# Modulation vectors by plain float32 matmuls in four 32-column strips, with nine early weight blocks in flight

## The chip, the core and the metric

The kernel runs on one core of a Trainium2 chip. Its engines are TensorE (PE, with its weight loads shown apart as PEld), VectorE (DVE), ScalarE (ACT), GpSimd (POOL) and SyncE (SP, which issues the transfers). Each engine takes its instructions in the order in which they were written for it, and waits for others through semaphores. The metric is device microseconds of one execution; lower is better.

## The reference, cut to what matters

Two layers of a generator's backbone run over 1024 latent tokens and 256 context tokens of width 1024. Each layer begins with a modulation: two conditioning vectors (one for the latents, `c`, one for the context, `c_ctx`) go through silu and a 1024 x 3072 weight, and give a shift, a scale and a gate per feature. The normed tokens are scaled and shifted with them before the layer's big input projection.

```python
for l in range(DEPTH):                      # DEPTH = 2
    mod = jax.nn.silu(c) @ w_mod[l] + b_mod[l]
    modc = jax.nn.silu(c_ctx) @ w_mod[l] + b_mod[l]
    shift, scale, gate = jnp.split(mod[:, None, :], 3, axis=-1)
    shift_c, scale_c, gate_c = jnp.split(modc, 3, axis=-1)
    h = rmsnorm(x, g_pre[l]) * (1.0 + scale) + shift
    hc = rmsnorm(xc, g_pre[l]) * (1.0 + scale_c) + shift_c
    u, uc = even_mixer(h, hc, ...) if l % 2 == 0 else odd_mixer(h, hc, ...)
    x = x + gate * rmsnorm(u @ w_out[l], g_post[l])
```

## The kernel before

**Products in float32r.** A matmul of the type fp32r streams a column per step of PE, but keeps fewer bits of its operands. So the kernel splits every operand of its large products into a high and a low part, and adds three products (high x high, high x low, low x high). A weight block is 128 x 1024 numbers, 512 KB. `load_w` (L223) has SP fetch it into `wraw`; `split_w` has ACT cast it into `whi` (L237) and POOL, or for some blocks DVE, subtract that from `wraw` into `wlo` (L238).

**The stream of weights.** `Stream` holds the weight blocks (`Unit`) in the order of their use. When a unit begins, `prefetch` loads the next three and splits the next one. There are three buffers for `wraw` and two for `whi` and `wlo`. The units of the first modulation (`early`) have a pool of their own, with four raw and three split buffers; six of them are loaded and two split ahead.

**The modulation.** `mod_units` computes 256 columns of one layer's modulation from two units of 512 x 256 numbers. `sst` holds the two silu vectors split in high and low, four columns for each of eight groups of 128 rows; it is the stationary operand (128 x 128, of which four columns matter), and the weight block is the moving one. A step (one unit) is eight fp32r matmuls of 256 columns, four on `whi` and four on `wlo` (L264), into one PSUM tile `modps`, whose rows 0 to 3 are the sums. `mod_flush` runs inside the next step or projection chunk: twice it copies four rows of 128 to SBUF (`modrow`, L282, DVE) and transposes them on PE (`modtr`, L283), then it adds them into columns (L285, L288). The layer's eight shift and scale blocks of layer 0 (16 units) come at the very start; the other 16 blocks (32 units: layer 0's gates, all of layer 1) stand in layer 0's stream, two blocks for each of the eight heads.

**The start.** `start` loads the first four token tiles, then the 16 modulation blocks, then further token tiles between the first weights of the projections. `make_h` turns the normed tokens into `h`: for each group of 128 features four transposes (`xtr`, L344), scale and shift (`ht`, L350 on DVE or L348 on ACT), cast (`hAh`, L351, ACT), subtraction (`hAl`, L352, DVE or POOL). Part A of `h` is tokens 0 to 511; part B (`hBh`, `hBl`) is tokens 512 to 1023 and the 256 of the context. The first projections (`pj`, L433; 24 matmuls for a chunk of tokens) start when A is there, and B is made beside them. DVE and POOL also turn the first results with the rotary tables (`ropex`).

**Layer 0's heads.** For each head, score matmuls (`S`), a softmax, transposes of the weights (`atr`, L606, evacuated by ACT and by DVE into `ath` and `atl`, L610) and value matmuls (`av`) are woven with the projections of the next head and of a convolution (`cacc`: L661 scales 1280 columns on DVE, L664 and L665 add the neighbours).

**What sets the order.** A scheduler of the kernel language decides, by its own estimates, in which order the instructions of each engine are written; after that the order is fixed. Outside the start and the neighbourhoods of the modulation steps in the eight heads, the change leaves that order as it was.

Of the kernel before, what the change touches and what calls it, by code (L numbers as in the profile page):

```python
# [31 lines left out]
class Unit:  # L32
    """a weight tile and the steps of the tensor engine that use it."""

    def __init__(self, name, src, steps, width=P, lo=None, pool=None):
        self.name, self.src, self.steps, self.width, self.lo_eng, self.pool = name, src, list(steps), width, lo, pool
        self.raw = self.hl = None
        self.hold = self.extra = False
        self.early = pool is not None


class Stream:
    """the weights in the order of their use: loaded two tiles ahead, split into hi and lo one tile ahead.
    A plain string in the order is a gate that stays shut until open() is called with it."""
# [4 lines left out]
    def ahead(self, n):  # L49
        """the next n units."""  # L50
        while sum(isinstance(u, Unit) for u in self.q) < n:
            u = next(self.units, None)
            if u is None:
                break
            self.q.append(u)
        return [u for u in self.q if isinstance(u, Unit)][:n]

    def prefetch(self, n=1):
        for i, u in enumerate(self.ahead(7)):
            if i < (6 if u.early else 3):  # L60
                self.K.load_w(u)
            if i < (2 if u.early else n):
                self.K.split_w(u)
# [37 lines left out]
class Kernel:  # L101
# [20 lines left out]
    def setup(self):  # L122
# [21 lines left out]
        self.sst = c.tile([P, 4 * NK + 124], F32R, name="sst")  # L144
# [15 lines left out]
    def turn_small(self, pool, rows, cols, name):  # L160
        """pieces of 128 numbers, each a row, into columns."""
# [10 lines left out]
    def setup_cond(self, p):  # L172
        """silu of the two conditioning vectors, split: columns c_hi, ctx_hi, c_lo, ctx_lo of each k."""
# [4 lines left out]
        sil = p.tile([P, 16], F32, name="sil")  # L178
        self.silu2(sil, self.colsA[:, 0:16])
        nc.vector.tensor_scalar_mul(sil, sil, 0.5)  # L180
        nc.vector.memset(self.sst.bitcast(F32), 0.0)
        sv = sil.rearrange("p (s k) -> p k s", s=2)
        s4 = self.sst[:, 0:4 * NK].rearrange("p (k s) -> p k s", s=4)
        nc.vector.tensor_copy(s4[:, :, 0:2], sv)
        nc.vector.tensor_tensor(out=s4[:, :, 2:4], in0=sv, in1=s4[:, :, 0:2].bitcast(F32), op=ALU.subtract)

    def setup_rest(self, p):
# [4 lines left out]
        # halves for the gates, which come as 2 silu  # L192
# [15 lines left out]
    def silu2(self, out, x):  # L208
        """2 silu(x) = x (1 + tanh(x / 2))."""
# [15 lines left out]
    def w_room(self, u, what=0):  # L225
        pool, *bufs = (self.prepw, 4, 3) if u.pool else (self.wp, 3, 2)
# [14 lines left out]
    def units(self):  # L241
        """every weight tile in the order of its use."""
        for j in (0, 4, 1, 5, 2, 6, 3, 7):
            yield from self.mod_units(0, j, "vp", (True, j > 3))
# [7 lines left out]
    def mod_units(self, l, j, lo=None, prep=None):  # L252
        """columns 256 j .. 256 j + 256 of mod(l), for latents and context."""
        st = {}

        def step(i):
            def f(hi, lo):
                nc = self.nc
                if i == 0:
                    st["ps"] = self.ps_pj.tile([P, 512], F32, name="modps", tag="pj")  # L260
                ps = st["ps"]
                for n, w in enumerate((hi, lo)):
                    for k in range(4):
                        nc.tensor.matmul(ps[:, 0:256], lhsT=self.sst[:, 16 * i + 4 * k:16 * i + 4 * k + P], rhs=w[:, k, :],  # L264
                                         start=i + n + k == 0, stop=i == n == 1 and k == 3)
                self.mod_flush()
                if i == 1:
                    self.mod_todo = (l, j, ps)
            return f

        for i in range(2):
            yield Unit(f"mod{l}.{j}.{i}", self.A["w_mod"][l][512 * i:512 * i + 512, 256 * j:256 * j + 256], [step(i)], 256, lo and lo[i], prep and prep[i])

    def mod_flush(self):
        """the last block's sums into columns."""
        if self.mod_todo is None:
            return
        nc, (l, j, ps), self.mod_todo = self.nc, self.mod_todo, None
# [23 lines left out]
    def rstd(self, r, t, ms, scale=1.0):  # L302
        """r from scale ms, with a step of Newton's behind the two tables; t is scratch."""
# [1303 lines left out]
```

## Time and profile before

| | |
|---|---|
| median of three runs | 3145.3 us (3143.07 to 3146.52) |
| span of the profiled execution | 3144.7 us |
| PE busy | 2961.4 us, 94% of the span |
| DVE, ACT, POOL busy | 62%, 49%, 35% |
| first projection matmul | 61.03 us |
| modulation matmuls | 384, of 256 columns |

PE is busy almost throughout, apart from the first 105 us. "Busy" of a matmul includes its way through the array, so that consecutive ones overlap: the distance between starts says what one costs. The granted clock is given in shares of full speed, 2.4 GHz; 0.50 is the lower level, 1.2 GHz.

### The profile page before, as it was taken

The page shows a single profiled execution, that of the slowest core. Times are in us where ns is not written, and L with a number is a line of the kernel's source. Part 1 is how long each engine was busy: PE and PEld are TensorE (multiplying, and loading weights), DVE is VectorE, ACT ScalarE, POOL GpSimd, SP SyncE. Part 2 cuts the span into 40 slices and gives each one's busy share as a digit, 9 for nine tenths or more (in the row PEclk, how much of TensorE's full clock was granted, in tenths as well). Part 3 has the DMA queues.
Part 4 walks back from the last instruction along what each step waited for, and adds up shares of the span by engine and source line. Part 5 has one row for each costly group of instructions (what it writes and reads, how often), then busy time and mean ns, then how long its engine had stood idle before and what let it go on. Part 6 is the DMA issues. An engine that isn't in the chain of part 4 may idle for free. (4 is left out here: it accounts for less than half of the span.)

```text
span 3144.7 us, 42660 instructions
## 1 busy us (share of the span) xinstructions
PE 2961.4 (94%) x16196; PEld 2480.0 (79%) x16196; DVE 1954.2 (62%) x3352; ACT 1547.3 (49%) x2809; POOL 1109.3 (35%) x851
## 2 busy tenths in 40 slices
PE   5999999999999999999999989989899999999898
PEld 4788888888888888787877777777778888887786
DVE  6774756656575757566254586776845666667723
ACT  5553535444454535464254465655534555556521
POOL 4323131212222231315233243443435555556522
PEclk8999999999999999999999999999999999999999
DMA  6011111102111111114343112121231111113323
GB/s 223 28 41 51 34 58 41 51 28 64 34 52 39 43 49 34 49 43 174 118 141 108 44 33 63 38 71 38 68 99 40 43 43 43 43 44 95 105 97 121
DMA packets 236983, 206.59 MB, mean 66 GB/s; under 512 B 43591, under 2 KB 194538, under 8 KB 236778
## 3 DMA queue, kind: packets, MB, share of 16 engines
q1 hardware_dynamic: 236778, 203.87, 20.7%
q8 instruction: 127, 2.08, 0.3%
q14 instruction: 78, 0.64, 0.1%
HBM read 168.17 MB, written 35.67 MB: 65 GB/s over the span
## 5 line engine op out<-in xcount | busy, mean ns | idle before, releaser
L238 POOL TENSOR_TENSOR wlo<-wraw,whi 128x1024 fp32r<-128x1024 f32 x189 | 459.6, 2434 | 1123.9 <-ACT whi L237 842.5
L237 ACT CAST whi<-wraw 128x1024 fp32r<-128x1024 f32 x224 | 234.5, 1049 | 327.7 <-PE ops L748 175.1
L433 PE MATMUL pj<-hBh,whi 128*128 128x512 f32 (+1 forms) x1712 | 386.0, 353 | 1.0 <-ACT gk L1035 1.0
L433 PE MATMUL pj<-hBl,whi 128*128 128x512 f32 (+1 forms) x1712 | 366.2, 346 | 0.0
L433 PE MATMUL pj<-hBh,wlo 128*128 128x512 f32 (+1 forms) x1712 | 353.3, 344 | 0.0
L433 PEld LDWEIGHTS pj<-hBh,wlo 128*128 128x128 f32 x1712 | 278.9, 190 | 37.4
L433 PEld LDWEIGHTS pj<-hBl,whi 128*128 128x128 f32 x1712 | 276.0, 190 | 34.6
L433 PEld LDWEIGHTS pj<-hBh,whi 128*128 128x128 f32 x1712 | 273.8, 190 | 34.3 <-ACT gk L1035 1.2
L433 PE MATMUL pj<-hAh,whi 128*128 128x512 f32 x968 | 275.5, 408 | 15.0 <-ACT ropex L511 11.9
L433 PE MATMUL pj<-hAl,whi 128*128 128x512 f32 x968 | 258.6, 398 | 0.0
L586 DVE TENSOR_REDUCE st<-S 128x1 f32<-128x1280 f32 (+1 forms) x160 | 203.9, 1275 | 80.5 <-PE S L584 79.4
L433 PE MATMUL pj<-hAh,wlo 128*128 128x512 f32 x968 | 248.2, 392 | 0.0
L1438 POOL TENSOR_TENSOR np<-np,nst 128x640 f32<-128x640 f32 x128 | 166.6, 1304 | 192.2 <-DVE nst L1437 143.7
L588 ACT ACTIVATE p<-S,st 128x1280 f32<-128x1280 f32 (+1 forms) x160 | 185.9, 1162 | 85.9 <-DVE st L586 85.1
L433 PEld LDWEIGHTS pj<-hAh,wlo 128*128 128x128 f32 x968 | 179.7, 188 | 36.3
L433 PEld LDWEIGHTS pj<-hAl,whi 128*128 128x128 f32 x968 | 180.2, 191 | 35.5
L433 PEld LDWEIGHTS pj<-hAh,whi 128*128 128x128 f32 x968 | 171.6, 191 | 44.2 <-ACT ropex L511 13.5
L584 PE MATMUL S<-kst,qd 128*128 128x512 f32 (+1 forms) x832 | 194.1, 363 | 0.6 <-ACT p L588 0.2
L584 PEld LDWEIGHTS S<-kst,qd 128*128 128x128 f32 x832 | 140.4, 191 | 40.2 <-ACT p L588 19.1
L1434 DVE CUSTOM_DVE_ANT_0 np<-NS,nB 128x640 f32<-128x640 f32 x128 | 105.3, 823 | 91.2 <-PE NS L1431 85.3
L609 ACT CAST ath<-atr 128x512 fp32r<-128x512 f32 (+1 forms) x208 | 99.1, 504 | 125.8 <-PE atr L606 124.8
L1489 DVE TENSOR_TENSOR ptl<-ntr,pth 128x512 fp32r<-128x512 f32 (+2 forms) x224 | 117.5, 536 | 49.0 <-ACT pth L1488 45.1
(361 smaller groups left out, 6384.2 us busy)
## 6 DMA issues: line engine op xcount, KB each, us to landing
wraw<-in_ev_w_in_dram SPq DMA_DIRECT2D x64, 512.0 KB, 4.1
wraw<-in_od_w_in_dram SPq DMA_DIRECT2D x56, 512.0 KB, 3.9
wraw<-in_w_out_dram SPq DMA_DIRECT2D x55, 512.0 KB, 3.7
wraw<-in_w_mod_dram SPq DMA_DIRECT2D x48, 512.0 KB, 3.6
sgT<-gt SPq DMA_DIRECT2D x32, 256.0 KB, 2.0
uT<-sg SPq DMA_DIRECT2D x8, 640.0 KB, 2.9
nG<-in_rpbp_dram SPq DMA_DIRECT2D x128, 40.0 KB, 2.2
xt<-in_x_dram SPq DMA_DIRECT2D x8, 512.0 KB, 6.2
```

Source lines behind the costliest of these rows:

```text
L237: nc.scalar.copy(out=hi, in_=u.raw)
L238: (nc.vector if u.lo_eng == "v" else nc.gpsimd).tensor_tensor(out=lo, in0=u.raw, in1=hi.bitcast(F32), op=ALU.subtract)
L433: nc.tensor.matmul(ps[:, 0:tn], lhsT=a[:, k, :], rhs=self.h_at(k, t0, tn)[b], start=n == 0, stop=n == 23)
L584: nc.tensor.matmul(S[:, c0:c0 + tn], lhsT=qd[:, 2 * m + part, P * qt:P * qt + P], rhs=self.kst[m][:, t0:t0 + tn], start=part == 0, stop=pa ...
L586: nc.vector.tensor_reduce(out=st[:, m:m + 1], in_=S[:, 0:n], axis=AX.X, op=ALU.max, negate=True)
L588: nc.scalar.activation(out=p[m][:, 0:n], in_=S[:, 0:n], func=AF.Exp, bias=st[:, m:m + 1], accum_out=st[:, 2 + m:3 + m])
L609: nc.scalar.copy(out=dh, in_=tv)
L1434: nc.vector.tensor_tensor_reduce(out=p, in0=S[:, z0:z0 + 640], in1=bias[2 * i + m][:, c0:c0 + 640], scale=1.0, scalar=3e38, op0=ALU.add, o ...
L1438: nc.gpsimd.tensor_tensor(out=p, in0=p, in1=st[:, 2:3].broadcast_to([P, 640]), op=ALU.mult)
L1489: nc.vector.tensor_tensor(out=lv[:, s:e], in0=tr[:, s:e], in1=hv[:, s:e].bitcast(F32), op=ALU.subtract)
```

## The change

The modulation's units become `plain`: they are not split. The raw float32 block is the moving operand of float32 matmuls. `sst` now holds, for each of the eight groups of 128 rows, 32 columns of which two are the silu vectors and 30 are zero. A step is four matmuls with a stationary operand of 32 columns; the k-th writes to PSUM partitions 32 k to 32 k + 31, that is, it takes the k-th strip of 32 columns of the array. The two steps of a block accumulate, strip by strip. DVE then copies all 128 rows at once (128 x 256), and two float32 matmuls with that copy as the stationary operand and `sel` (128 x 2; column s is one on the rows 32 k + s) as the moving one add the four strips and turn rows into columns. The copy stands at the end of a block's second step, the two matmuls ahead of the next step's (or behind the next projection chunk's). The early units get nine raw buffers and eight are loaded ahead.

```diff
     def prefetch(self, n=1):
-        for i, u in enumerate(self.ahead(7)):
-            if i < (6 if u.early else 3):
+        for i, u in enumerate(self.ahead(9)):
+            if i < (8 if u.early else 3):
                 self.K.load_w(u)
-            if i < (2 if u.early else n):
+            if i < n and not u.early:
                 self.K.split_w(u)
...
+        self.sel = c.tile([P, 2], F32, name="sel")
+        nc.vector.tensor_reduce(out=self.sel, in_=self.ident.rearrange("p (j x) -> p x j", x=32)[:, 0:2, :], axis=AX.X, op=ALU.add)
...
+    def new_sst(self, pool, eng):
+        self.sst = pool.tile([P, NK, 32], F32, name="sst")
+        eng.memset(self.sst, 0.0)
+        eng.tensor_copy(self.sst[:, :, 0:2], self.sil)
...
-        pool, *bufs = (self.prepw, 4, 3) if u.pool else (self.wp, 3, 2)
+        pool, *bufs = (self.prepw, 9, 0) if u.early else (self.wp, 3, 2)
...
+        if u.plain:
+            u.hl = u.raw.rearrange("p (k n) -> p k n", n=u.width),
+            return
...
-            def f(hi, lo):
+            def f(w):
                 nc = self.nc
+                self.mod_flush()
                 if i == 0:
                     st["ps"] = self.ps_pj.tile([P, 512], F32, name="modps", tag="pj")
                 ps = st["ps"]
-                for n, w in enumerate((hi, lo)):
-                    for k in range(4):
-                        nc.tensor.matmul(ps[:, 0:256], lhsT=self.sst[:, 16 * i + 4 * k:16 * i + 4 * k + P], rhs=w[:, k, :],
-                                         start=i + n + k == 0, stop=i == n == 1 and k == 3)
-                self.mod_flush()
+                for k in range(4):
+                    nc.tensor.matmul(ps[32 * k:32 * k + 32, 0:256], lhsT=self.sst[:, 4 * i + k, :], rhs=w[:, k, :], start=i == 0, stop=i == 1)
                 if i == 1:
-                    self.mod_todo = (l, j, ps)
+                    row = self.rowp.tile([P, 256], F32, name="modrow", tag="modrow")
+                    nc.vector.tensor_copy(row, ps[:, 0:256])
+                    self.mod_todo = (l, j, row)
...
         for i in range(2):
-            row = self.const.tile([16, P], F32, name="modrow", tag="modrow")[0:4]
-            nc.vector.tensor_copy(row, ps[0:4, P * i:P * i + P])
-            nc.tensor.transpose(out=tr[:, 4 * i:4 * i + 4], in_=row, identity=self.ident[0:4, 0:4])
-        tc_ = self.const.tile([P, 8], F32, name="modtc", tag="modtc", bufs=2)
-        nc.vector.tensor_copy(tc_, tr[:, 0:8])
-        for i in range(2):
-            m = 2 * j + i
-            nc.vector.scalar_tensor_tensor(out=self.modT[l][:, m, :], in0=tc_[:, 4 * i:4 * i + 2], scalar=self.b_mod(l)[:, m:m + 1],
-                                           in1=tc_[:, 4 * i + 2:4 * i + 4], op0=ALU.add, op1=ALU.add)
+            nc.tensor.matmul(tr[:, 2 * i:2 * i + 2], lhsT=row[:, P * i:P * i + P], rhs=self.sel, start=True, stop=True)
+        m = slice(2 * j, 2 * j + 2)
+        nc.vector.tensor_tensor(out=self.modT[l][:, m, :], in0=tr[:, 0:4].rearrange("p (m s) -> p m s", s=2),
+                                in1=self.b_mod(l)[:, m].rearrange("p (m o) -> p m o", o=1).broadcast_to([P, 2, 2]), op=ALU.add)
```

PE's order at the start, before (line 264 is a modulation matmul, 283 a transpose of its sums, 344 a transpose of tokens):

```order
L264 MATMUL modps<-whi,sst 128x256 x4
L264 MATMUL modps<-wlo,sst 128x256 x4
L264 MATMUL modps<-whi,sst 128x256 x4
L264 MATMUL modps<-wlo,sst 128x256 x4
L264 MATMUL modps<-whi,sst 128x256 x4
L264 MATMUL modps<-wlo,sst 128x256 x4
L283 MATMUL modtr<-ident,modrow 128x4
L264 MATMUL modps<-whi,sst 128x256 x4
L283 MATMUL modtr<-ident,modrow 128x4
```

The same place in the changed kernel (line 271 is a modulation matmul, 290 the sum of the strips, 348 a transpose of tokens):

```order
L271 MATMUL modps<-wraw,sst 32x256 x8
L290 MATMUL modtr<-sel,modrow 128x2 x2
L271 MATMUL modps<-wraw,sst 32x256 x8
L290 MATMUL modtr<-sel,modrow 128x2 x2
L348 MATMUL xtr<-ident,xt 128x128 x4
L271 MATMUL modps<-wraw,sst 32x256 x8
L290 MATMUL modtr<-sel,modrow 128x2 x2
```

The sums of a block now stand directly behind its second step, with nothing between for PE to do while DVE copies; this holds for the first five blocks, and the last three run as one row of 24 matmuls.

PE's order in the first head, before, where the first block's two steps stand behind eight transposes of attention weights:

```order
L606 MATMUL atr<-ident,p_1598 128x128 x8
L264 MATMUL modps<-whi,sst 128x256 x4
L264 MATMUL modps<-wlo,sst 128x256 x4
L264 MATMUL modps<-whi,sst 128x256 x4
L264 MATMUL modps<-wlo,sst 128x256 x2
L606 MATMUL atr<-ident,p_1598 128x128 x2
L264 MATMUL modps<-wlo,sst 128x256 x2
L433 MATMUL pj<-hAh,whi 128x512 x4
```

The same place in the changed kernel (lines 437 and 611 are 433 and 606 of before):

```order
L611 MATMUL atr<-ident,p_1431 128x128 x8
L271 MATMUL modps<-wraw,sst 32x256 x8
L437 MATMUL pj<-hAh,whi 128x512 x3
L611 MATMUL atr<-ident,p_1431 128x128 x2
L437 MATMUL pj<-hAh,whi 128x512 x3
```

Three matmuls of the next projection have moved ahead of the last two transposes. The other block's two steps of a head, some 35 us later, stand in the changed kernel in groups of one, three and four matmuls between transposes and value matmuls.

POOL's order in the first head, before (238 is the subtraction for `wlo`, 675 a part of the convolution, 535 a copy of queries), from the copies of the queries to the convolution's gate:

```order
L535 COPY qf<-ropex 128x512
L238 TENSOR_TENSOR wlo<-wraw,whi 128x1024
L535 COPY qf<-ropex 128x256
L238 TENSOR_TENSOR wlo<-wraw,whi 128x1024 x9
L675 TENSOR_TENSOR cacc<-cacc,csg 128x512 x2
```

and in the changed kernel (lines 540, 244 and 680 are the same operations):

```order
L540 COPY qf<-ropex 128x512
L244 TENSOR_TENSOR wlo<-wraw,whi 128x1024
L540 COPY qf<-ropex 128x256
L244 TENSOR_TENSOR wlo<-wraw,whi 128x1024 x5
L680 TENSOR_TENSOR cacc<-cacc,csg 128x512 x2
```

Four subtractions of 128 x 1024 have left POOL's row for this head.

## Rows read from the trace of the kernel before

**Rows 1.** The page: span; a group of instructions (busy us, mean ns, idle before).
```profile
span 3144.7 us, 42660 instructions
...
L238 POOL TENSOR_TENSOR wlo<-wraw,whi 128x1024 fp32r<-128x1024 f32 x189 | 459.6, 2434 | 1123.9 <-ACT whi L237 842.5
```
**Rows 2.** Stretches: length, PE, PEld, DVE, ACT, POOL busy, clock, DMA share, GB/s.
```profile
40.00:60.00 20.00, 13.29 (x69) 11.09 (x67) 15.34 (x36) 13.05 (x19) 9.48 (x5) 0.70 0.88 303
60.00:80.00 20.00, 15.02 (x72) 11.19 (x72) 13.05 (x23) 12.57 (x20) 9.09 (x8) 0.91 0.26 73
80.00:105.00 25.00, 20.55 (x100) 16.20 (x100) 24.59 (x40) 13.09 (x26) 11.60 (x11) 0.93 0.00 0
```
**Rows 3.** Timeline of ACT, 12.9 to 18 us (start, duration, instruction, idle before).
```profile
12.97 1.04 ACT L237 CAST whi<-wraw 128x1024 fp32r<-128x1024 f32 x1 [0.29 <-DMA wraw<-in_w_mod_dram]
14.48 1.05 ACT L237 CAST whi<-wraw 128x1024 fp32r<-128x1024 f32 x1 [0.47 <-DMA wraw<-in_w_mod_dram]
```
**Rows 4.** Groups of DVE, 0 to 62 us: busy us, mean ns, idle before.
```profile
L238 DVE TENSOR_TENSOR wlo<-wraw,whi 128x1024 fp32r<-128x1024 f32 x8 | 13.8, 1727 | 0.2 <-ACT whi L237 0.2
L288 DVE SCALAR_TENSOR_TENSOR modT<-modtc,colsA 128x2 f32<-128x2 f32 x14 | 12.1, 897 | 0.1
```
**Rows 5.** Timelines of DVE and POOL, 62 to 69 us.
```profile
64.41 2.50 DVE L288 SCALAR_TENSOR_TENSOR modT<-modtc,colsA 128x2 f32<-128x2 f32 x2
...
64.42 2.34 POOL L238 TENSOR_TENSOR wlo<-wraw,whi 128x1024 fp32r<-128x1024 f32 x1
```
**Rows 6.** Timelines of ACT and PE: tiles 6 and 7 scaled, first context chunk.
```profile
69.10 2.18 ACT L385 ACTIVATE xt<-xt,r 128x1024 f32<-128x1024 f32 x2
...
103.15 1.11 PE L433 MATMUL pj<-hBh,whi 128*128 128x256 f32 x8
```
**Rows 7.** First head, timelines of POOL and DVE; then line 661 (min/median/max ns).
```profile
187.17 2.38 POOL L238 TENSOR_TENSOR wlo<-wraw,whi 128x1024 fp32r<-128x1024 f32 x1 [22.50 <-ACT whi L237]
...
187.43 2.81 DVE L661 TENSOR_SCALAR cacc<-cw,colsB 128x1280 f32<-128x1280 f32 x1
...
L661 DVE TENSOR_SCALAR cacc<-cw,colsB x8: 2815/2816/2986, 187.4 to 1423.2; 128x1280 f32<-128x1280 f32 x8
```
**Rows 8.** Timeline of PE in the first head, 191.4 to 197 us.
```profile
192.28 0.72 PE L264 MATMUL modps<-whi,sst 128*128 128x256 f32 x4
...
193.79 0.39 PE L264 MATMUL modps<-wlo,sst 128*128 128x256 f32 x2
195.99 0.44 PE L606 MATMUL atr<-ident,p 128*128 128x128 f32 x2 [1.81 <-DVE atl L610]
196.51 0.85 PE L433 MATMUL pj<-hAh,whi 128*128 128x512 f32 x3
```
**Rows 9.** Stretches as in rows 2, behind such waits of two later heads.
```profile
540.00:543.40 3.40, 3.40 (x11) 2.81 (x12) 1.28 (x5) 3.21 (x5) 1.90 (x2) 0.50 0.39 116
714.10:717.50 3.40, 3.40 (x10) 2.73 (x9) 0.71 (x5) 2.47 (x4) 2.20 (x1) 0.50 0.53 154
```
**Rows 10.** Plain float32 matmuls of the heads' norm: timeline, then PE's groups by shape.
```profile
233.65 1.02 PE L630 MATMUL ms<-qf,onesD 128*128 128x512 f32 x2
...
L630 PE MATMUL ms<-qf,onesD 128*128 128x512 f32 x32 | 16.4, 593 | 0.0
```
**Rows 11.** Timeline of PE around a transpose of sums, 206.5 to 207.4 us.
```profile
206.72 0.28 PE L620 MATMUL av<-atl,vh 128*128 128x256 f32 x1
206.93 0.22 PE L283 MATMUL modtr<-ident,modrow 4*128 4x4 f32 x1
207.08 0.39 PE L620 MATMUL av<-ath,vl 128*128 128x256 f32 x1
```
**Rows 12.** Timeline of PE around a 16-column stationary operand, late in the kernel.
```profile
2974.45 0.28 PE L1456 MATMUL nav<-ptl,nv 128*128 128x256 f32 x1
2974.57 0.27 PE L758 MATMUL ggtr<-ident,ggc 128*16 128x128 f32 x1
2974.59 0.48 PE L748 MATMUL ops<-whi,uAh 128*128 128x512 f32 x1
```

More of the change, by code (lines that the diff above doesn't have):

```diff
@@ L32, with __init__ @@
 class Unit:
-    def __init__(self, name, src, steps, width=P, lo=None, pool=None):
-        self.name, self.src, self.steps, self.width, self.lo_eng, self.pool = name, src, list(steps), width, lo, pool
+    def __init__(self, name, src, steps, width=P, lo=None, plain=False):
+        self.name, self.src, self.steps, self.width, self.lo_eng, self.plain = name, src, list(steps), width, lo, plain
         self.raw = self.hl = None
-        self.hold = self.extra = False
-        self.early = pool is not None
+        self.hold = self.extra = self.early = False
 class Stream:
@@ L177, in setup_cond @@
                             v(A["b_mod"], "l (k p) -> (l k) p")], self.colsA, "A")
-        sil = p.tile([P, 16], F32, name="sil")
+        sil = p.tile([P, 16], F32, name="silc")
         self.silu2(sil, self.colsA[:, 0:16])
[L180 to L185, printed above, removed]
+        nc.vector.tensor_scalar_mul(self.sil, sil.rearrange("p (s k) -> p k s", s=2), 0.5)
+        self.new_sst(self.prepw, nc.vector)
+    def new_sst(self, pool, eng):
+        self.sst = pool.tile([P, NK, 32], F32, name="sst")
+        eng.memset(self.sst, 0.0)
+        eng.tensor_copy(self.sst[:, :, 0:2], self.sil)
     def setup_rest(self, p):
@@ L243, in units @@
         for j in (0, 4, 1, 5, 2, 6, 3, 7):
-            yield from self.mod_units(0, j, "vp", (True, j > 3))
+            yield from self.mod_units(0, j, True)
         yield "layer0"
@@ L261, in f @@
                 ps = st["ps"]
-                for n, w in enumerate((hi, lo)):
-                    for k in range(4):
-                        nc.tensor.matmul(ps[:, 0:256], lhsT=self.sst[:, 16 * i + 4 * k:16 * i + 4 * k + P], rhs=w[:, k, :],
-                                         start=i + n + k == 0, stop=i == n == 1 and k == 3)
-                self.mod_flush()
+                for k in range(4):
+                    nc.tensor.matmul(ps[32 * k:32 * k + 32, 0:256], lhsT=self.sst[:, 4 * i + k, :], rhs=w[:, k, :], start=i == 0, stop=i == 1)
                 if i == 1:
-                    self.mod_todo = (l, j, ps)
+                    row = self.rowp.tile([P, 256], F32, name="modrow", tag="modrow")
+                    nc.vector.tensor_copy(row, ps[:, 0:256])
+                    self.mod_todo = (l, j, row)
             return f
         for i in range(2):
-            yield Unit(f"mod{l}.{j}.{i}", self.A["w_mod"][l][512 * i:512 * i + 512, 256 * j:256 * j + 256], [step(i)], 256, lo and lo[i], prep and prep[i])
+            u = Unit(f"mod{l}.{j}.{i}", self.A["w_mod"][l][512 * i:512 * i + 512, 256 * j:256 * j + 256], [step(i)], 256, plain=True)
+            u.early = early
+            yield u
     def mod_flush(self):
@@ L277, in mod_flush @@
             return
-        nc, (l, j, ps), self.mod_todo = self.nc, self.mod_todo, None
+        nc, (l, j, row), self.mod_todo = self.nc, self.mod_todo, None
         tr = self.ps_tr.tile([P, 512], F32, name="modtr", tag="tr")
         for i in range(2):
-            row = self.const.tile([16, P], F32, name="modrow", tag="modrow")[0:4]
-            nc.vector.tensor_copy(row, ps[0:4, P * i:P * i + P])
-            nc.tensor.transpose(out=tr[:, 4 * i:4 * i + 4], in_=row, identity=self.ident[0:4, 0:4])
-        tc_ = self.const.tile([P, 8], F32, name="modtc", tag="modtc", bufs=2)
-        nc.vector.tensor_copy(tc_, tr[:, 0:8])
-        for i in range(2):
-            m = 2 * j + i
-            nc.vector.scalar_tensor_tensor(out=self.modT[l][:, m, :], in0=tc_[:, 4 * i:4 * i + 2], scalar=self.b_mod(l)[:, m:m + 1],
-                                           in1=tc_[:, 4 * i + 2:4 * i + 4], op0=ALU.add, op1=ALU.add)
+            nc.tensor.matmul(tr[:, 2 * i:2 * i + 2], lhsT=row[:, P * i:P * i + P], rhs=self.sel, start=True, stop=True)
+        m = slice(2 * j, 2 * j + 2)
+        nc.vector.tensor_tensor(out=self.modT[l][:, m, :], in0=tr[:, 0:4].rearrange("p (m s) -> p m s", s=2),
+                                in1=self.b_mod(l)[:, m].rearrange("p (m o) -> p m o", o=1).broadcast_to([P, 2, 2]), op=ALU.add)
     def mod_finish(self, l, what, k0=0, k1=NK):
@@ L365, in start @@
             w_es = ExitStack()
-            self.prepw = self.pool("prepw", ctx=w_es)
+            self.prepw = self.rowp = self.pool("prepw", ctx=w_es)
             pq = self.pool("ps_sq", space=PSUM, ctx=es)
@@ L495, in layer0 @@
         conv_es = ExitStack()
-        self.cp = self.pool("conv", ctx=conv_es, side="right")
+        self.cp = self.rowp = self.pool("conv", ctx=conv_es, side="right")
+        self.new_sst(self.cp, self.nc.gpsimd)
         with ExitStack() as es2:
```

4 lines of the change are left out of this document (2 added, 2 removed).

## The prediction

> **What bounds the kernel now.** I read the stretches first. From about 105 us on, PE is the bound: it is busy in 94% of the span, and the order of its work does not change. Ahead of that it is not: in the stretches from 40 to 60 and 80 to 105 us [rows 2] PE is busy two thirds and four fifths of the time. From 80 to 105 us DVE is busy 24.6 of 25 us, and no byte is transferred: the second half of `h` is made there, at DVE's pace. What lies before it is the modulation. The casts of ACT follow each other at 1.5 us, each behind a transfer [rows 3], as long as there are raw buffers; then the splitting holds the blocks back. In the first 62 us DVE spends 13.8 us on eight subtractions (1.73 us each) and 12.1 us on fourteen additions of two columns (0.9 us each) [rows 4]. The timelines say why: an addition of two columns begins at 64.41 and ends with POOL's subtraction, which runs from 64.42 to 66.76 [rows 5]. DVE stands still beside POOL's 128 x 1024 subtraction. So the view to read next is where else that happens: in each of the eight heads the scaling of 1280 columns (line 661) takes 2.8 us. In the first head it ends at 190.24, 0.69 us after POOL's subtraction, which ended at 189.55 [rows 7]; without POOL it would take about these 0.7 us (an estimate). A few us later PE waits 1.81 us for DVE [rows 8], within the first block's modulation steps. Seven heads have this wait.
>
> **The change: the start.** The modulation needs no split any more, so a block is ready when its transfer has landed. Sixteen blocks at 1.5 us from 12.97 on [rows 3] have landed at 35.5; nine buffers never hold SP back, since PE is then less than nine blocks behind. SP's order stays the same, so that token tiles 4 to 7 and one weight block (512 KB each, five times 1.5) have landed at 43.0. Squares, root and scaling take the last two tiles to about 49.5: 1.2 us for squares, 2 us for the root, 2.2 us for scaling [rows 6], and one foreign square between. Before, the scaling ended at 71.28 [rows 6].
> PE may be later than that. Call t the time of one step of four strip matmuls. Each of the first five blocks takes 2 t, then 0.8 us in which PE waits for DVE's copy, 0.5 us for the two matmuls that add the strips and 0.45 us for four transposes; the last three blocks take 6 t in a row. With t = 1.2 that is 20.8 + 7.2 = 28.0 us, and 2.4 us more for a first block at the lower clock: from 13 us on, the modulation ends at 43.4. The last two tiles of `h` and the 24 matmuls of the first chunk (0.225 us each) take some 8.5 us, so that the second half of `h` starts at 52, not at 71.3. From there it took 31.9 us to the first chunk of the context (103.15) [rows 6], at DVE's pace, with the same work afterwards. The gain is 19.5 us, say **20**. If t is at its smallest the tiles bound it (49.5) and it is 23; each 0.1 us of t more costs 1.6.
>
> **The change: t, which no row shows.** A plain float32 matmul of the heads' norm is two passes of 512 columns; each lasts 0.593 us by the groups and the two together 1.02, so that they start 0.43 us apart [rows 10], 0.21 for 256 columns. A step is eight such passes. One end: the strips take turns, eight times 0.21, t = 1.71. The other end: four strips stream at once, two passes, t = 0.43. I take a staircase: the passes start in order, the two of one strip share its columns and follow each other, but the first of the next strip runs beside the second of this one, as they share neither columns nor PSUM partitions. That is five passes, 1.07, and 0.13 for entering and leaving; **t = 1.2**, near the middle of the two ends. Weight loads of 32 columns I count as hidden, as the full ones are.
> Entering a narrow stationary operand costs nothing in the one place that shows it: the 16-column one (line 758) starts 0.12 us after a matmul of 256 columns, as any neighbour would [rows 12]. The Trainium skill (TensorEngine Tiling (Array Packing), Key Properties) says that changing the tiling mode drains the array; rows 12 show no such drain, but whether that operand counts as a strip they cannot say. The same page says that tiles work independently, and TensorE: Matmul & The Clock Gate (Part 3, Measured speedup vs the span model) gives 2.38 times for three column tiles; no row here shows strips side by side, and by that figure, as an estimate, four would be at or below my 1.2.
>
> **The change: the eight heads.** (a) First block of a head: from the first modulation matmul to the next projection's first is 4.23 us (192.28 to 196.51), with the wait of 1.81 [rows 8]. After: two steps 2.4 and two transposes 0.3. The wait goes, because the subtraction at 187.17 was a modulation block's and is gone, which gives DVE 2.1 us back. What is late next is PE itself. Gain 1.5. (b) The second block: sixteen matmuls at 0.12 [rows 12], 1.9 us; after 2.4. Loss 0.5. (c) The sums: a transpose of four rows stretches the distance between its neighbours from 0.12 to 0.36 (206.72 to 207.08), and the next load of 0.1 is not hidden [rows 11]: 0.35 each, four per head, 1.4 us. After: four matmuls of two passes, each as long as a load of 128 columns (about 0.11), 0.9 to 1.0. Gain 0.4. Per head 1.4, in seven heads **10**; the eighth has no such wait and I count nothing.
> Behind three of these waits the granted clock stood at 0.50 for 3.4 us, the lower level [rows 9]; at the full one that work takes half. Without the waits I count three times 1.7 = **5**.
> ACT loses 48 casts and POOL 40 subtractions of 2.43 us [rows 1]; beyond what is named they hide beside PE, and are worth nothing. DVE's copy of 128 x 256 replaces two small copies and four small operations. The raw block now stays until PE is done with it, and SP's next transfer waits for that; two blocks of a head lie some 30 us apart, which covers a transfer of 4 us.
>
> **Sum.** 20 + 10 + 5 = 35 from the profiled 3144.7, 3109.7; the median of the runs lies 0.6 above that execution: **3110 us**.
>
> **Rivals.** *Turns*, t = 1.71: the start gives 12, a head loses (a) gains 0.5, (b) loses 1.5, (c) gains 0.4: 0.6, 5 in all; clock 3. 3145.3 - 10 = 3135. For it: the passes of rows 10 strictly follow each other. Against: they share all columns. *At once*, t = 0.43: start 23; (a) bounded by DVE, 2.2, (b) 1.1, (c) 0.4, 26 in all; clock 5: 3091. Against it: the two passes of a strip stand next to each other. *Drains*: if each entry into strips and back costs what the transpose of four rows does beyond its share, 0.29 us, then four groups a head (eight, one, three, four matmuls) cost 9 and the start 2: 3121. Rows 11 speak for it, rows 12 against. *The wait stays*: the subtraction of the next projection block falls upon another of DVE's operations ahead of the transposes, the heads gain nothing and the clock still drops: 3125. For it: POOL keeps eight subtractions a head; against: they now stand after the scaling in the order. *Loads not hidden* is the one on the slow side: if each pass waits for its own load (0.19 as PE's loads last, plus 0.21, eight times), t = 3.2; the start loses 12 instead of gaining 20, a head loses 2.5 + 4.5 - 0.4 = 6.6, 53 in all: 3145.3 + 65 = 3210. The point from which it decides: the sum falls by 46 us for each us of t (16 steps at the start, 30 in the stream), so 35 are used up at t = 1.96.
>
> **How the numbers follow.** Staircase (3100 to 3118) 45%, turns 17%, drains 10%, at once 10%, the wait stays 8%, loads not hidden 10%. The range reaches from *at once*, less 5 for the start, 3086, to *turns* plus 7, 3142; it leaves out the slow case and some of the edges. A measurement of this kernel tells about 0.2% from no change, 6.3 us. Faster by more: all but the slow case and the weaker part of *turns*, 0.82; within it 0.08; slower 0.10.
>
> **What would show it.** Right: the casts and subtractions of modulation blocks gone; modulation matmuls over by 45 us; first context chunk at 80 to 86 us; line 666 (661 before) at 0.7 us; no wait of 1.8 us on `atl`; passes of neighbouring strips starting less than 0.21 us apart, or overlapping. Wrong: steps of 1.7 us or more, PE's idle time moving to the copy of the sums in the heads, or a start that still ends behind 95 us because DVE, not the tiles, sets it.

## The result, and the profile after

The changed kernel took 3089.2 us in the median of four runs (3086.7 to 3091.2), the kernel before 3144.2: a ratio of 0.983, 95% interval 0.981 to 0.984. The gain is 55 us; 35 were forecast. The time lies in the stated range and near its lower end, outside the band of the likeliest case (3100 to 3118) and at the price of the rival *at once* (3091).

The profiled execution has a span of 3087.9 us (3144.7 in [rows 1]). From the page (span; a group's busy us, mean ns, idle before):

```profile
span 3087.9 us, 42515 instructions
...
L244 POOL TENSOR_TENSOR wlo<-wraw,whi 128x1024 fp32r<-128x1024 f32 x149 | 367.0, 2463 | 1097.3 <-ACT whi L243 1017.0
```

The view of single lines (count, min/median/max ns of one, first and last start, operands):

```profile
L271 PE MATMUL modps<-wraw,sst x384: 379/379/636, 12.7 to 1369.8; 128*32 128x256 f32 x192
...
L666 DVE TENSOR_SCALAR cacc<-cw,colsB x8: 871/886/887, 170.6 to 1367.0; 128x1280 f32<-128x1280 f32 x8
```

Forty subtractions of POOL are gone [rows 1]. The scaling of 1280 columns takes 0.89 us where it took 2.82 [rows 7].

**The start.** The timelines of ACT and PE (start, duration, instruction, idle before it and what ended that):

```profile
53.96 2.19 ACT L389 ACTIVATE xt<-xt,r 128x1024 f32<-128x1024 f32 x2 [1.98 <-DVE r L329]
...
31.48 2.80 PE L271 MATMUL modps<-wraw,sst 128*32 128x256 f32 x48
36.17 0.25 PE L171 MATMUL trB<-ident,rowsB 35*128 35x35 f32 x1 [1.89 <-DMA rowsB<-in_ev_conv_dram]
...
42.92 0.77 PE L437 MATMUL pj<-hAh,whi 128*128 128x512 f32 x1
...
83.34 0.87 PE L437 MATMUL pj<-hBh,whi 128*128 128x256 f32 x6
85.67 0.69 PE L437 MATMUL pj<-hBh,whi 128*128 128x256 f32 x2 [1.45 <-ACT hBh L355]
...
88.80 0.51 PE L437 MATMUL pj<-hBl,whi 128*128 128x256 f32 x2 [0.90 <-DVE hBl L356]
```

The modulation's last strip matmuls are over at 34.3, and the first chunk of the context begins at 83.34, 19.8 us before its old place [rows 6]. The two waits behind it are new, and of the 19.8 us 16.8 are left from 107 us on (the same projection matmuls in both traces).

**A head.** Timelines of PE in the first head. The second fence begins with a window of 0.04 us:

```profile
175.64 1.07 PE L271 MATMUL modps<-wraw,sst 128*32 128x256 f32 x16
176.64 0.97 PE L437 MATMUL pj<-hAh,whi 128*128 128x512 f32 x3
```

```profile
206.73 0.42 PE L271 MATMUL modps<-wraw,sst 128*32 128x256 f32 x4
...
204.04 0.62 PE L271 MATMUL modps<-wraw,sst 128*32 128x256 f32 x2
...
205.85 0.63 PE L271 MATMUL modps<-wraw,sst 128*32 128x256 f32 x6
206.42 0.38 PE L625 MATMUL av<-ath,vh 128*128 128x256 f32 x1
206.73 0.64 PE L271 MATMUL modps<-wraw,sst 128*32 128x256 f32 x8
207.30 0.74 PE L437 MATMUL pj<-hAh,whi 128*128 128x512 f32 x2
```

The first row of the second fence says that four passes of 256 columns start within 0.04 us: the four strips run side by side. A step of eight passes takes 0.57 us from its first pass to the next other instruction, three matmuls take 0.57 as well, and one takes 0.55 (from 204.04 to the next instruction at 204.59). Two steps in a row take 1.00. So a further step costs 0.43, and the rest is the way in and out. The first block's stretch of 4.23 us [rows 8] has become 1.0; no wait stands in it, and the two transposes that stood in it now come 0.8 us later.

What PE waited for between 175 (192 in before) and 1390 us, first before, then after (in total, times, longest):

```profile
PE atr L606 <- DVE atl L610: 13.5, 12, 1.8
PE pj L433 <- ACT ropex L511: 11.9, 8, 2.4
PE atr L606 <- DVE p L594: 5.5, 7, 0.8
PE modtr L283 <- DVE modrow L282: 2.6, 7, 0.4
PE pj L433 <- DVE csg L212: 1.5, 6, 0.3
```

```profile
PE pj L437 <- ACT ropex L516: 13.0, 7, 5.3
PE S L589 <- ACT p L593: 0.2, 1, 0.2
```

All waits for DVE are gone, 23.1 us of them. The first row of before is the wait that the prediction spoke of; the third and fourth it had left out. The waits for ACT's copy of the projections' results (`ropex`) sum up to much the same, but one of them is now 5.3 us long:

```profile
1234.68 3.78 PE L437 MATMUL pj<-hAh,whi 128*128 128x512 f32 x8 [5.29 <-ACT ropex L516]
```

PE had done nothing since 1229.4, and the granted clock stands at 0.50 from 1231.9 to 1238.8.

**The account.** The first modulation step of the first head starts at 175.64 (192.28 in before, [rows 8]), that of the eighth head at 1333.99 (1388.60 in before). Between the two lie seven heads: 1196.3 us before, 1158.35 after. Summed over PE's records in this stretch (a matmul costs the distance to the next one's start, less that one's wait):

| us in seven heads | before | after | gain |
|---|---|---|---|
| PE waits | 36.8 | 13.9 | 23.0 |
| modulation steps | 30.7 | 18.8 | 11.9 |
| sums of the strips | 4.7 | 5.1 | -0.4 |
| everything else | 1124.1 | 1120.6 | 3.5 |

The last row is for the most part the clock. The stretches that stood at 0.50 [rows 9] run at full clock now; the third of them is 1058.8 to 1062.2. PE's work in the three was 9.4 us, so that this gives 4.7. The new stretch behind the wait of 5.29 us holds 4.3 us of PE's work and takes 2.1 back. The other 0.9 us is the balance of small gains and losses that were not traced one by one. One loss among them: the first projection matmul behind strips takes 0.34 us to the next start (176.64 to 176.98), the one after it 0.24. The row below is one of the three stretches, after:

```profile
540.00:543.40 3.40, 3.40 (x31) 2.78 (x30) 2.65 (x7) 1.82 (x5) 0.00 (x0) 1.00 0.56 152
```

With the eighth head the gain stands at 58 us at 1500; it ends one lower, and the spans differ by 56.8.

### The profile page after: what moved, and what is told of

Read it like the earlier page. It is cut to its first block, busy times and chain, and to the rows that moved or that the text cites. A ratio compares the mean times of both kernels' runs of the same rounds, so it can differ in the third digit from the quotient of the medians.

```text
span 3087.9 us, 42515 instructions
## 1 busy us (share of the span) xinstructions
PE 2935.2 (95%) x16244; PEld 2439.3 (79%) x16244; DVE 1910.7 (62%) x3272; ACT 1503.5 (49%) x2761; POOL 1027.9 (33%) x813
## 5 line engine op out<-in xcount | busy, mean ns | idle before, releaser
L244 POOL TENSOR_TENSOR wlo<-wraw,whi 128x1024 fp32r<-128x1024 f32 x149 | 367.0, 2463 | 1097.3 <-ACT whi L243 1017.0
L243 ACT CAST whi<-wraw 128x1024 fp32r<-128x1024 f32 x176 | 184.5, 1048 | 321.3 <-PE ops L753 193.7
L437 PEld LDWEIGHTS pj<-hBh,wlo 128*128 128x128 f32 x1712 | 277.2, 190 | 36.8
```

The lines of the kernel that those rows point to most:

```text
L243: nc.scalar.copy(out=hi, in_=u.raw)
L244: (nc.vector if u.lo_eng == "v" else nc.gpsimd).tensor_tensor(out=lo, in0=u.raw, in1=hi.bitcast(F32), op=ALU.subtract)
L437: nc.tensor.matmul(ps[:, 0:tn], lhsT=a[:, k, :], rhs=self.h_at(k, t0, tn)[b], start=n == 0, stop=n == 23)
```

## The experiments

Each kernel is named with its median and its ratio to the kernel before, measured beside it. The changed kernel's ratio is 0.983, and 0.001 is 3.1 us. A ratio's interval is about 0.0015 either way, so that differences below 0.003 between two kernels rest on the traces.

### What the strips do

**Without strips.** The stationary operand is 128 columns wide and the eight matmuls of a block accumulate.

```diff
-                    nc.tensor.matmul(ps[32 * k:32 * k + 32, 0:256], lhsT=self.sst[:, 4 * i + k, :], rhs=w[:, k, :], start=i == 0, stop=i == 1)
+                    g = 4 * i + k
+                    nc.tensor.matmul(ps[:, 0:256], lhsT=self.sst[:, 2 * g:2 * g + P], rhs=w[:, k, :], start=g == 0, stop=g == 7)
```

> Plain float32 without strips: the stationary operand is 128 columns wide, of which two matter, and the eight matmuls of a block accumulate in the same rows. Nothing is split. Theory S (the strips run side by side, and that is what makes a step 0.43 us): a step takes eight passes of 0.216, 1.73 us, without the 0.19 that entering and leaving the strips costs; a head loses 4.6 us (4 steps by 1.3, less three groups by 0.19), 37 in all, the start up to 8: 3126 to 3134 us. Rival (plain float32 passes of few useful columns overlap anyhow, or the steps hide beside other waits): less than 10 us above the changed kernel, below 3100.

3130.8 us, ratio 0.996 (0.994 to 0.997): 41 us above the changed kernel. Its timeline of PE in the first head:

```profile
180.64 1.89 PE L272 MATMUL modps<-wraw,sst 128*128 128x256 f32 x8
182.37 0.41 PE L612 MATMUL atr<-ident,p 128*128 128x128 f32 x2
```

Eight passes take 1.73 us to the next instruction, four times the 0.43. Theory S holds. PE waits for DVE 0.4 us in all of its heads, so that the loss there is PE's own: the modulation steps of seven heads take 25 us more. Some 5 of the 41 us lie in the start; the rest was not traced. This is the rival *turns*, t = 1.73 for its 1.71, and 3131 us for its 3135.

**Two strips a step.** 

```diff
-                    nc.tensor.matmul(ps[32 * k:32 * k + 32, 0:256], lhsT=self.sst[:, 4 * i + k, :], rhs=w[:, k, :], start=i == 0, stop=i == 1)
+                    s = 2 * i + k // 2
+                    nc.tensor.matmul(ps[32 * s:32 * s + 32, 0:256], lhsT=self.sst[:, 4 * i + k, :], rhs=w[:, k, :], start=k % 2 == 0, stop=k % 2 == 1)
```

> The same eight matmuls of a block, but a step uses two strips, two matmuls behind each other on each: first step strips 0, 0, 1, 1, second step 2, 2, 3, 3. The sums are the same. Theory Q (each strip takes its passes in its own turn, and a strip's waiting pass does not hold the passes of the next): four passes deep, 0.86 us a step and not 0.43; 32 steps in the heads make 14 us, the start 0 to 4: 3101 to 3108. Rival, the staircase of the prediction (the passes start in order, so that the second strip begins only beside the last pass of the first): seven passes, 1.5 us, 34 us in the heads: 3123 and up. Rival, nothing follows anything: no change.

3095.9 us, ratio 0.984 (0.983 to 0.986): half of what theory Q said. Its timeline shows why:

```profile
176.59 1.09 PE L272 MATMUL modps<-wraw,sst 128*32 128x256 f32 x16
177.61 0.74 PE L438 MATMUL pj<-hAh,whi 128*128 128x512 f32 x2
...
208.16 1.06 PE L272 MATMUL modps<-wraw,sst 128*32 128x256 f32 x8
209.15 0.73 PE L438 MATMUL pj<-hAh,whi 128*128 128x512 f32 x2
```

A step that stands alone takes 0.99 us, not 0.57: 0.42 more, as four passes in a strip instead of two. But two steps in a row (x16) still take 1.02: the second step's strips 2 and 3 run beside the first's 0 and 1, although the first's second matmuls on strips 0 and 1 stand ahead of them in the program. Four passes start within 0.04 us of the first (176.59), on four strips, and the next ones on the same strips 0.24 us later. So a pass that waits for its strip does not hold up those of other strips, over a whole step. That is theory Q's mechanism; its sum was wrong, since it charged all 32 steps and only those of the second block (two of a head's four) pay: 16 by 0.42 are 6.7 us, and 0.984 less 0.983 is about that. The staircase of the prediction would have cost 34.

**Three times the matmuls in the stream.**

```diff
-                for k in range(4):
-                    nc.tensor.matmul(ps[32 * k:32 * k + 32, 0:256], lhsT=self.sst[:, 4 * i + k, :], rhs=w[:, k, :], start=i == 0, stop=i == 1)
+                for n in range(1 if early else 3):
+                    for k in range(4):
+                        nc.tensor.matmul(ps[32 * k:32 * k + 32, 0:256], lhsT=self.sst[:, 4 * i + k, :], rhs=w[:, k, :],
+                                         start=i == n == 0, stop=i == 1 and (early or n == 2))
```

> In the stream's 32 steps the four strip matmuls are issued three times over (the gates' and the second layer's modulation come out three times too large; the start is as in the changed kernel). 64 further groups of four. Theory Q (each strip takes its own passes in its own turn, the four side by side): 0.43 us each, 28 us above the changed kernel, 3112 to 3122, some us of it open since the order of the work around moves. Staircase of the prediction (1.07 without the entry): 68 us, 3150 to 3165. Turns (1.73): 3200.

3124.1 us, ratio 0.994 (0.992 to 0.995): 35 us for 64 further groups, 0.54 each; theory Q said 28, and its range ended at 3122. The order moved and cut the rows into more pieces, each with its way in and out. Where a row is long, 26 passes take 1.84 us (to the next instruction at 177.33):

```profile
175.49 1.91 PE L272 MATMUL modps<-wraw,sst 128*32 128x256 f32 x26
```

These are thirteen matmuls, four of them on the first strip: its eight passes in turn, seven distances of 0.22 and the 0.31 behind the last, make 1.85. Q again; the staircase's 68 us are excluded.

### What POOL's subtractions do

**Casts and subtractions kept.** The stream's blocks are split for nobody.

```diff
         if u.plain:
             u.hl = u.raw.rearrange("p (k n) -> p k n", n=u.width),
+            if not u.early:
+                hi, lo = self.w_room(u, 1)
+                nc.scalar.copy(out=hi, in_=u.raw)
+                nc.gpsimd.tensor_tensor(out=lo, in0=u.raw, in1=hi.bitcast(F32), op=ALU.subtract)
             return
```

> The stream's 32 modulation blocks stay plain on PE, but each is still cast by ACT and subtracted by POOL into buffers that nobody reads, so that the two engines have their work of before back. Theory A (a part of the gain in the heads is POOL's subtraction, beside which DVE stands still, so that PE waits for DVE: 1.81 and 0.78 us in each of seven heads of the kernel before, and the clock falls behind three of the waits): such waits come back in most heads, 12 to 25 us above the changed kernel, 3101 to 3114 us. Theory B (the gain is PE's own: fewer and shorter instructions): within 5 us of the changed kernel, 3084 to 3094.

3143.2 us, ratio 0.999 (0.998 to 1.000): nothing of the gain is left. Both theories are wrong in size, B in kind. PE's waits in the heads, then ACT and PE in the first of them:

```profile
PE atr L615 <- DVE atl L619: 31.3, 14, 3.5
...
PE atr L615 <- DVE p L603: 7.7, 7, 1.1
```

```profile
149.45 1.05 ACT L243 CAST whi<-wraw 128x1024 fp32r<-128x1024 f32 x1 [2.22 <-POOL wlo L244]
152.99 1.05 ACT L247 CAST whi<-wraw 128x1024 fp32r<-128x1024 f32 x1 [2.50 <-POOL wlo L244]
...
154.22 1.06 ACT L618 CAST ath<-atr 128x512 fp32r<-128x512 f32 x2
...
156.89 0.44 PE L615 MATMUL atr<-ident,p 128*128 128x128 f32 x2 [2.87 <-DVE atl L619]
```

Here a second route shows: there are two split buffers, ACT's next cast waits until POOL has done with one, and ACT's copies of the attention weights (`ath`) are queued behind the cast. DVE gets them late, and PE waits 2.87 us. In two later waits of each head DVE itself had stood still (the scaling, now line 670, takes 2.77 us again). Of the 52 us, 39 are waits for DVE by the rows above: by the trace, seven behind ACT's casts (2.9 us, in the last head 3.5; 20.7 together), seven of 1.5 us behind the scaling and seven of 1.1 us behind a cast of queries on which DVE stood still too. The records of everything else are 10.9 us longer in the seven heads. That is the clock: PE works 25.1 us of them at the lower level, in the changed kernel 4.3, and half of the difference is 10.4. Five of these stretches (the first from 330.0 to 333.4) begin within 2 us of a wait of 2.9 us.

**Casts alone**, POOL's line left out; PE's order is that of the run above but for a few places.

> As the run with casts and subtractions kept, but with ACT's casts alone; POOL's subtractions of modulation blocks are gone. Theory A (POOL holds DVE up): no more than 5 us above the changed kernel, 3084 to 3094. Rival (ACT's 32 casts of 1.05 us delay the copies out of PSUM that PE waits for): 8 us or more above it, 3097 and up.

3087.4 us, ratio 0.982 (0.980 to 0.983), the same as the changed kernel. ACT's 32 casts cost nothing, as the prediction said.

**A copy of POOL in place of the subtraction**, every engine in the order of the first of these runs.

```diff
-                nc.gpsimd.tensor_tensor(out=lo, in0=u.raw, in1=hi.bitcast(F32), op=ALU.subtract)
+                nc.gpsimd.tensor_copy(out=lo, in_=hi.bitcast(F32))
```

> As the run with casts and subtractions kept, in the same order on every engine, but POOL copies the cast block where it subtracted (half the operands; its copy of 128 x 512 took 0.61 us, its subtraction of 128 x 1024 2.4). Two routes are open by which POOL's subtraction cost 54 us in that run: DVE stands still beside it, and ACT's next cast waits for the split buffers that it holds, with the copies out of PSUM queued behind. Theory A (both go with POOL's time and its operands): a copy of about 1.2 us leaves a third or less of the 54 us, 3089 to 3107. Rival (any work of POOL at this place costs the same, whatever it is): 3130 and up.

3092.7 us, ratio 0.984 (0.982 to 0.985). The groups of POOL and of DVE:

```profile
L244 POOL CAST wlo<-whi 128x1024 fp32r<-128x1024 f32 x32 | 33.3, 1040 | 380.1 <-ACT whi L243 380.1
...
L670 DVE TENSOR_SCALAR cacc<-cw,colsB x8: 1407/1409/2350, 171.7 to 1369.4; 128x1280 f32<-128x1280 f32 x8
```

With 1.04 us of POOL at the same places instead of 2.4, the waits for DVE sum up to 2.4 us and almost the whole loss is gone. So it is not that POOL works there at all: DVE is still held up (its scaling takes 1.41 us, not 0.89), but by too little for PE to wait. The copy is shorter and has one operand, and this run does not tell the two apart.

**Subtractions without casts.** POOL subtracts the raw block from itself; ACT has no part in it, and PE, DVE and ACT keep the changed kernel's order.

```diff
+            if not u.early:
+                hi, lo = self.w_room(u, 1)
+                nc.gpsimd.tensor_tensor(out=lo, in0=u.raw, in1=u.raw, op=ALU.subtract)
```

> The changed kernel, with PE's, DVE's and ACT's order unchanged, and 32 subtractions more on POOL (a raw modulation block less itself, into a buffer that nobody reads), without casts. ACT waits for nothing of it, so only the stand-still of DVE is left of the two routes. Theory A (DVE's stand-still is what costs): waits of PE for DVE come back in most heads, 10 to 30 us above the changed kernel, 3099 to 3119. Rival (ACT's queue was the route by which the casts and subtractions cost 54 us): less than 5 us above it, 3087 to 3094.

3107.2 us, ratio 0.988 (0.986 to 0.990): 18 us above the changed kernel, as theory A said. Its DVE, POOL and PE:

```profile
170.92 2.16 DVE L669 TENSOR_SCALAR cacc<-cw,colsB 128x1280 f32<-128x1280 f32 x1
180.33 1.88 DVE L599 TENSOR_TENSOR st<-st,neglam 128x1 f32<-128x1 f32 x1
...
170.51 1.89 POOL L243 TENSOR_TENSOR wlo<-wraw 128x1024 fp32r<-128x1024 f32 x1 [18.50 <-PE pj L440]
180.29 1.89 POOL L243 TENSOR_TENSOR wlo<-wraw 128x1024 fp32r<-128x1024 f32 x1 [7.89 <-DMA wraw<-in_w_mod_dram]
...
178.84 0.44 PE L614 MATMUL atr<-ident,p 128*128 128x128 f32 x2 [0.90 <-DVE atl L618]
185.88 1.44 PE L592 MATMUL S<-kst,qd 128*128 128x512 f32 x6 [1.49 <-ACT p L596]
```

DVE's scaling ends 0.68 us after POOL's subtraction (172.40 and 173.08), as in [rows 7], and seven heads have the wait of 0.9 us behind it. In five heads a second subtraction begins at the same time as a DVE operation on a single column (`st`), which takes 1.8 to 1.9 us (0.15 in the changed kernel, at 178.74). The softmax on ACT needs its result, and PE waits 1.4 to 1.5 us for ACT. These two waits are 13.6 us in seven heads, by as much as all of PE's waits there grow (27.5 for 13.9). So the stand-still alone is worth 18 us in this order. How the 52 us of the first run divide between the two routes in that other order is read from its trace alone (20.7 us of its waits behind ACT's casts, 18.3 behind DVE); no run takes out ACT's route by itself.

**The kernel before, without the low parts of the stream's modulation blocks.**

```diff
+        if u.name.startswith("mod") and not u.early:
+            lo = hi
+        else:
             (nc.vector if u.lo_eng == "v" else nc.gpsimd).tensor_tensor(out=lo, in0=u.raw, in1=hi.bitcast(F32), op=ALU.subtract)
```

> The kernel before, in whose stream the 32 modulation blocks get no low part: POOL's subtraction is left out, and the matmuls on the low part read the high part again (so their modulation comes out about twice as large); PE's instructions, the start and ACT's casts are those of before. Theory A (most of the gain in the heads is POOL's subtraction): the waits of 1.81 and 0.78 us in seven heads, and the time at the lower clock behind three of them, go: 20 to 27 us below the kernel before, 3117 to 3125. Rival (the gain in the heads is PE's own shorter work): less than 8 us below it, 3136 to 3144.

3133.2 us, ratio 0.996 (0.995 to 0.997): 12 us below the kernel before, between the two theories. PE's instructions are those of before, but not all in its order: behind the first block of a head, score matmuls now stand ahead of the next projection. Its waits:

```profile
PE atr L609 <- DVE p L597: 5.8, 7, 0.8
PE modtr L286 <- DVE modrow L285: 2.6, 7, 0.4
```

The wait of 1.8 us is gone, and so is the lower clock behind it. The other two stay. The wait of 0.8 us comes beside a projection block's subtraction: POOL has one at 230.95 here, at 232.66 in before, and none between 207.5 and 222 of the changed kernel, where the same place is. So by the traces that part of the gain came from where POOL's remaining work fell; no run moved it alone.

### The start

**Four early buffers.** 

```diff
-            if i < (8 if u.early else 3):
+            if i < (6 if u.early else 3):
...
-        pool, *bufs = (self.prepw, 9, 0) if u.early else (self.wp, 3, 2)
+        pool, *bufs = (self.prepw, 4, 0) if u.early else (self.wp, 3, 2)
```

> The early blocks get four raw buffers, six are loaded ahead, as before the change; all else as in the changed kernel, in the same order on every engine. Theory A (the transfers bound the first 35 us, and PE takes a block within some 2 us of its landing, so that four buffers nearly do): 0 to 4 us above the changed kernel, 3088 to 3094. Rival (the nine buffers carry the start's gain of 17 us): 8 us or more, 3097 and up.

3097.7 us, ratio 0.985 (0.984 to 0.987). SP's and PE's timelines:

```profile
4.69 29.37 SPq L226 DMA_DIRECT2D wraw<-in_w_mod_dram  x16
34.11 0.97 SPq L380 DMA_DIRECT2D xt<-in_x_dram  x2
...
38.87 1.08 PE L271 MATMUL modps<-wraw,sst 128*32 128x256 f32 x8 [2.77 <-DMA wraw<-in_w_mod_dram]
...
90.22 0.76 PE L437 MATMUL pj<-hBh,whi 128*128 128x256 f32 x5
```

Theory A is wrong: SP is held behind the blocks until 34.1 (26.4 with nine buffers), PE waits for transfers, and everything behind is 6.9 us later, which is what stays in the heads. So of the start's 17 us the buffers make 7, and the plain blocks 10. The rival had the buffers right in kind, but not as the whole.

**Small rows early.** 

```diff
             load_x(0, 4)
+            self.setup_rest(p)
             self.ws.run(1)
...
-                if j == 1:
-                    self.setup_rest(p)
```

> The small rows (convolution taps, norms, biases) are loaded and turned right behind the first four token tiles, not amid the modulation. In the changed kernel PE waits 1.89 us at 36.17 for these rows and 1.94 us at 38.89 for DVE's copy of them, with the last sums of the modulation behind it. Theory A (these waits are on the path to the first projection): 2 to 4 us below the changed kernel, 3085 to 3087. Rival (from 43 us on the last token tiles and DVE set the pace, whenever the modulation ends): within 1 us of it, 3088 to 3090.

3095.7 us, ratio 0.985 (0.983 to 0.986): slower, which neither theory foresaw. The rows no longer hold PE up, but the order of the start moved: the last three blocks, one row of 48 passes in the changed kernel, stand apart, and each waits for DVE's copy. They end at 42.6, not at 34.3. PE then waits for a cast and for the token tiles:

```profile
38.75 1.00 PE L290 MATMUL modtr<-sel,modrow 128*128 128x2 f32 x4 [1.85 <-DVE modrow L274]
...
40.64 1.94 PE L271 MATMUL modps<-wraw,sst 128*32 128x256 f32 x16
...
49.29 1.65 PE L436 MATMUL pj<-hAh,whi 128*128 128x512 f32 x3 [3.35 <-ACT whi L243]
54.17 0.69 PE L348 MATMUL xtr<-ident,xt 128*128 128x128 f32 x2 [3.23 <-ACT xt L389]
...
90.46 0.76 PE L436 MATMUL pj<-hBh,whi 128*128 128x256 f32 x5
```

It does not tell the two theories apart, since it changed more than it meant to. No kernel that was run is measurably faster than the changed one.

## Why the prediction was right in its range and wrong in its size

**What bounds the kernel: right.** PE in the heads, DVE and the loads in the start, POOL's subtraction beside DVE as the cause of a wait. The wait of 1.8 us went, line 666 fell to 0.89 us (0.7 was said), and the clock stayed up where that wait had been.

**The start, 20: right at its own mark, by two errors that cancel.** The first chunk of the context came 19.8 us earlier, at 83.34 (80 to 86 was said). But the last token tiles were scaled at 56.2, not at 49.5 (52 was taken as the start of the second half): their root waited for DVE, which stood beside a projection block's subtraction (1.73 us from 50.83, POOL from 50.13 to 52.54). And the second half of `h` then took 27 us, not 32: DVE was busy 23.2 us in it, 27.8 in before, as four of seven operations on `kst` stood in it where all seven had. Three microseconds were lost again behind the mark, in the two waits for the context's `h`.

**t = 1.2: wrong, and the main error.** The step that failed is the staircase, "the first of the next strip runs beside the second of this one". The starts show all four strips' first passes within 0.04 us and the next ones 0.24 and then 0.22 later: t = 0.43 for a further step, and the two-strip run shows that a waiting pass holds up only its own strip. The argument against *at once*, that the two passes of a strip stand next to each other, was no obstacle: they follow each other on their strip and hold up no other. At 0.77 us a step this is 3.1 us a head, 25 us in eight; in the start it hid behind the transfers.

**Entering strips costs nothing: wrong, a small term.** A strip pass starts 0.20 us after a transpose, where a neighbour would start after 0.11, and a full-width matmul 0.31 after the last strip pass, not 0.22: 0.09 in and 0.09 out. [Rows 12], read as the price of strips, show nothing of it; what sets that operand of 16 columns apart was not tried. The Trainium skill (TensorEngine Tiling (Array Packing), Key Properties) says that changing the mode drains the array. A delay of 0.09 us each way fits that, but these rows can't show that it is a drain. The rival *drains* had the cost, at 0.29 too high, from the row transpose of [rows 11].

**The heads, 10: nearly four times as much.** In the first head PE's work behind the modulation is 5.4 us nearer (16.8 at its start, 22.2 at its end), not 1.4. (a) gave 2.3 (forecast 1.5). (b) and (c), together a loss of 0.1 in the forecast, gave the rest: the second block's steps became shorter, and two waits that the prediction had not listed went, 0.78 us for DVE's weights and 0.37 for the copy of the sums (5.5 and 2.6 us in seven heads by the table of waits). The reconciliation in eight heads: 10 as forecast, 25 for t, 8 for the two waits, less 6 for the way in and out (four groups a head by 0.18), are 37, and 3.5 from the last row of the account make 40; measured are 41 (16.8 at 170 us, 58 at 1500).

**The clock, 5: right for its three stretches**, 4.7 us; the new stretch at 0.50 behind the wait for `ropex`, which the prediction had not, takes 2.1 back. **ACT's casts, nothing: right**, by the run that kept them. **The rest of POOL's subtractions, nothing: not tested by itself.** Taking all of the stream's out of the kernel before gave 12 us, and the seven waits of 1.81 us, which the prediction counted, are 12.7. In the other orders that were run the same subtractions cost 18 and 52 us.

The range held because it reached to *at once*, a case that had a tenth of the chance. That the time lies in it is no merit of the staircase; that much was luck.

## What to carry to other kernels

Before pricing an operation at a middle between two ends, ask which end its resources allow: here four strips shared no columns and no partitions, and the end at which nothing is shared was the right one. List every wait in the stretch that a change touches, not only the longest, since a change that shifts the work takes the small ones with it. And price the work of an engine by the places where another must stand beside it: the same 32 subtractions cost 12, 18 and 52 us in three orders of the same work.

## What the runs showed of the hardware beyond that

- Plain float32 on four 32-column strips streams four passes of 256 columns in the 0.22 us of one: a step takes 0.43 us, and 1.73 with a full-width stationary operand. Only steps that stand together gain all of it: alone, a step costs 0.57, as much as three matmuls of it.
- PE starts a later strip's pass while an earlier instruction's pass still waits for its strip, across two steps of four matmuls (two passes each): in the two-strip run the second step's strips start 0.04 us behind the first's, and the first step's second matmuls 0.46 us behind.
- POOL's cast of 128 x 1024 takes 1.04 us, its subtraction of two different operands 2.4, of one operand from itself 1.89; beside either subtraction DVE's scaling ends 0.7 us after POOL, and an operation of DVE on one column took 1.88 us for 0.15.
